# Token mixing in a two-block transformer kernel: convolution taps between POOL and ACT, six chunks on the raw input, scores placed later

## The chip, the cores and the metric

The kernel runs on one core of a Trainium2 chip. The core has five engines that work side by side, each through its own row of instructions in a fixed order: PE (matrix products), DVE (vector), ACT (scalar functions), POOL (general elementwise work) and SP, which here only issues loads. They wait for each other through semaphores. The time that counts is the device time of one execution in microseconds (us).

## What is computed

Two blocks follow each other. The first has two layers of: gated feed-forward, token mixing, gated feed-forward, each followed by a layer norm. It works on 272 tokens (16 learned ones and 256) of 1024 channels. The second block (attention and state mixing with modulation) is not touched by the change. The token mixing, with what matters here:

```python
def token_mix(h, w_in, pool_w, pool_scale, conv_dw, conv_db, conv_ln_g, conv_ln_b, conv_pw, ret_gn_g, w_out):
    z = h @ w_in                                   # 2816 columns
    xp, ca, cg, q, k, v, g = jnp.split(z, splits, axis=-1)
    y_pool = pool_mixer(xp, pool_w, pool_scale)    # trailing means over 2, 4, 8, 16 tokens, minus xp, times pool_w
    y_conv = conv_module(ca, cg, conv_dw, ...)     # ca * sigmoid(cg), causal 31-tap depthwise convolution, norm, silu, product
    y_ret = retention(q, k, v, g, ret_gn_g)        # 4 heads of 128, rotated q and k, decayed scores, head norm, gate
    return jnp.concatenate([y_pool, y_conv, y_ret], axis=-1) @ w_out
```

## The kernel before

Channels lie on the 128 partitions, tokens along the free axis; the state is eight tiles `st` of 128 channels. Each product is made three times in a reduced format: weights and inputs are split into a rounded high part and a rest, and PE adds high x high, high x low and low x high (lines 147 to 149 in `mm3`). A weight chunk of 1024 x 128 is loaded by SP into `raw` (L134), ACT casts it to `whi` (L140) and DVE subtracts to get `wlo` (L141). So one chunk on PE is 8 x 3 = 24 products of 272 columns. Four PSUM buffers take chunks (`mm_ps`, the pool `pmm`), four others scores and the like (`aux_ps`).

`token_mix` runs through 22 chunks of `w_in` in the order of `W_IN_KINDS`, two chunks for each entry. The first `RAWT` chunks come from `raw_tiles`: PE multiplies the state as it is, scaled by the layer norm's gain alone (two columns more carry the sums that the mean and the bias need), while statistics and the norm itself are still being made. What comes out of PSUM is then corrected: ACT copies the two columns to `wb` (L188), DVE subtracts the mean's part into `rz` (L190), POOL multiplies with the reciprocal deviation (L191), and the bias is added by the user of the tile. Beside it `ln_apply` makes the normalised input tile by tile: DVE `st` and `lnu` (L306, L308), ACT the high half of `xb` (L314), DVE the low half (L315), POOL the new state (L316). The other chunks come from `tiles` (PSUM tile `ps_g`) and multiply that normalised input; the first two of them share a sweep over its eight tiles.

What is done with a chunk: `ca` and `cg` make the convolution's input `cu` (POOL L584 and L587, ACT tanh L588, DVE L589). From then on `conv_tap` is called five times per chunk, with a lower priority. The convolution's two channel tiles are treated differently: t = 0 goes to DVE, one fused instruction for each tap (L442); t = 1 goes to POOL, one instruction for the product into a tile `tap` (L446) and one to add it to `cy` (L447). `q` and `k` are rotated in `rope_ret`: ACT copies the two halves exchanged into a tile `sw` (L424, L425), DVE multiplies twice and adds (L426 to L428). When a head's key is there, `ret_scores` makes its scores on PE (`ps_s`, L510) and DVE multiplies them with the decay (L511). `xp` is copied by ACT (L603) and then pooled in `pool_mix`, a generator of POOL instructions (L455 to L469) that is advanced twice per chunk, with two products at its end (`ps_pool`, L473). `v` and `g` are copied; after chunk 17 the values are transposed, the outputs `ps_o` made (L622), the convolution's norm and product follow in `conv_out`, and after chunk 21 the gates and transposes in `ret_out`. The eight chunks of `w_out` end the mixing.

A scheduler sets the order on each engine at build time, from the order in which the program is written, priorities, and when buffers come free. Short-lived tiles made by `self.t` (`tap`, `sw`, `rz`, `lnu`, `th`, `sq` and others) share one tag of six buffers: who takes a seventh waits until the last reader of one is done. An instruction that waits holds up all that stand behind it on its engine.

The module's constants that the change touches:

```python
RAWT = 4
W_IN_KINDS = (("ca", 256), ("cg", 512), ("q", 768), ("k", 1280), ("q", 1024), ("k", 1536), ("xp", 0),
              ("v", 1792), ("v", 2048), ("g", 2304), ("g", 2560))
```

Of the kernel before, what the change touches and what calls it, by code (L numbers as in the profile page):

```python
# [14 lines left out]
AF = mybir.ActivationFunctionType  # L15
ALU = mybir.AluOpType
AX = mybir.AxisListType
PSUM = bass.MemoryType.PSUM
# [21 lines left out]
RAWT = 4  # L40
LATE = 11
ACC = {"s": 0, "q": 1, "x0": 0, "x1": 2, "y": 0, "w": 1, "xw": 2}
W_IN_KINDS = (("ca", 256), ("cg", 512), ("q", 768), ("k", 1280), ("q", 1024), ("k", 1536), ("xp", 0),
# [45 lines left out]
class Ker:  # L89
# [61 lines left out]
    def gemm(self, items, X, cols, mark=0, tail=0):  # L151
        """items: (PSUM tile, weight chunk) pairs that share the sweep over the rows of X, but for the last `tail` rows."""
# [15 lines left out]
    def raw_tiles(self, srcs, ln, lead=2):  # L168
        """As tiles, of a layer norm's output, from its input scaled by the gain alone.

        Yields SBUF tiles that lack only the channel's bias, and the bias; the norm itself is made on the way."""
# [28 lines left out]
    def tiles(self, srcs, X, cols, kt=KD, lead=4, segs=None, hold=()):  # L200
        """Yields PSUM tiles of X @ w, one per 128-column chunk; the first `lead` share a sweep over X,
        one for each of segs, column ranges that become ready one after the other."""
# [23 lines left out]
    def mean_b(self, group, d, n, name, ps=None):  # L226
        """Mean over the channels of a group of tiles, the same in each partition."""
# [12 lines left out]
    def sqrt_table(self, after=None):  # L240
        """Have the square root's table in place before the chain that needs it."""
# [6 lines left out]
    def acc(self, S, key, m, src, n, eng):  # L248
        """Running sum over channel tiles; the eighth stays apart for the matmul that ends it."""
# [31 lines left out]
    def ln_raw(self, S, i, m, z, n):  # L281
        """Split of z times the gain of layer norm i, for raw_tiles."""
# [11 lines left out]
    def ln_start(self, S, i, eps, n, off, X):  # L294
        """Mean and reciprocal deviation, the same in each partition."""
# [5 lines left out]
    def ln_apply(self, S, i, eps, n, off, X, M, R, c):  # L301
        """State tile c <- its layer norm i; X gets the split of it."""
# [42 lines left out]
    def ada_cols(self, l):  # L345
        """Per-channel factors of layer l, [128, 8, 2] with the last axis (x, ctx)."""
# [16 lines left out]
    def ffn1(self, l, f, X, raw, n, off, ln):  # L363
        """SwiGLU; state <- 2 alpha state + ffn(state), and the sums of it."""
# [55 lines left out]
    def rope_ret(self, ps, dst):  # L420
        """dst <- ps * cos + halves swapped * signed sin, channels on partitions."""
# [131 lines left out]
    def token_mix(self, l, X, raw, n, off, ln):  # L553
# [25 lines left out]
        for c, z in enumerate(chain(self.raw_tiles(srcs[:RAWT], raw), self.tiles(srcs[RAWT:], X, slice(0, L1), lead=2))):  # L579
            kind, m = W_IN_KINDS[c // 2][0], c % 2  # L580
            if m == 0 and kind not in ("ca", "cg"):
                dst = self.hid2(kind)
# [1032 lines left out]
```

## Time and profile before

| | us |
|---|---|
| median of three runs (2161.81 to 2168.8) | 2165.63 |
| span of the profiled execution, first to last instruction | 2156.3 |
| median less that span | 9.3 |
| first layer's token mixing (218.1 to 350) | 131.9 |
| second layer's (752.2 to 882.5) | 130.3 |

The profiled execution's time is given by its span alone; what lies around it (start and end of the program) is taken from the median. Times on the profile's axis begin with the first instruction. An instruction's row names the engine, the line, what is written and read, and how long it took; its duration counts also what it waited for after its start, such as another engine's hold on the memory's ports. A wait is put down to the engine that came last. The granted clock of PE is shown as a share of its full speed.

### The profile page before, as it was taken

How to read it: one execution, taken by the hardware profiler on the slowest of the kernel's cores; microseconds unless marked ns; L12 is line 12 of the kernel's file. 1: busy time of each engine (PE TensorE's matmuls, PEld its weight loads, DVE VectorE, ACT ScalarE, POOL GpSimd, SP SyncE). 2: the span in 40 equal slices, each digit the busy share in tenths (PEclk: the TensorE clock that was granted, in tenths of full speed). 3: DMA queues.
4: the chain of work that ended last, by engine and by line, in shares of the span. 5: the costliest groups of instructions: out<-in, count | busy, mean ns of one | idle time of the engine just before them, and what ended most of it. 6: DMA issues, size and time to landing. Idle time of an engine off the chain costs nothing.

```text
span 2156.3 us, 37011 instructions
## 1 busy us (share of the span) xinstructions
PE 2088.8 (97%) x14486; PEld 1920.0 (89%) x14486; DVE 1575.5 (73%) x2554; ACT 1097.3 (51%) x1870; POOL 466.4 (22%) x500
## 2 busy tenths in 40 slices
PE   7999889999999989999999999999999998999998
PEld 7999889999999978999988788888888888789998
DVE  8889898989897789887755546685435558568873
ACT  6444446544554445654546656554324455566663
POOL 5002795202500288600200000310000013211000
PEclk9999999999999999999999999999999999999999
DMA  8877334787587724587522211133243232024653
GB/s 275 271 238 270 100 121 160 245 268 242 175 283 252 253 99 130 159 290 252 186 91 91 69 50 36 44 99 87 76 121 93 69 103 87 22 78 137 185 178 109
DMA packets 96079, 328.38 MB, mean 152 GB/s; under 512 B 10912, under 2 KB 13600, under 8 KB 95648
## 3 DMA queue, kind: packets, MB, share of 16 engines
q1 hardware_dynamic: 95328, 325.45, 47.0%
q8 instruction: 114, 1.87, 0.3%
q10 hardware_dynamic: 576, 0.56, 0.1%
q14 instruction: 61, 0.50, 0.1%
HBM read 324.92 MB, written 1.05 MB: 151 GB/s over the span
## 4 chain that ended last, share of the span: by engine, by line
PE 82%; POOL 8%; DVE 6%; issue 3%; ACT 2%; DMA 0%; DVEq 0%; POOLq 0%; ACTq 0%
PE ps_g L147 14%; PE ps_g L148 13%; PE ps_g L149 13%; PE ps_y L147 4%; PE ps_y L148 4%; PE ps_y L149 4%; PE ps_d L149 3%; PE ps_d L147 3%; POOL cy L447 3%; PE ps_d L148 3%; POOL tap L446 2%; PE ps_o L1049 2%; PE ps_s L1414 1%; PE ps_r L147 1%; PE ps_r L149 1%
## 5 line engine op out<-in xcount | busy, mean ns | idle before, releaser
L140 ACT CAST whi<-raw 128x1024 fp32r<-128x1024 f32 (+2 forms) x527 | 535.2, 1017 | 607.7 <-issue 174.1
L141 DVE TENSOR_TENSOR wlo<-raw,whi 128x1024 fp32r<-128x1024 f32 (+2 forms) x527 | 633.9, 1212 | 250.8 <-ACT whi L140 247.6
L147 PE MATMUL ps_g<-xb,whi 128*128 128x272 f32 (+2 forms) x2320 | 707.1, 307 | 8.6 <-DVE rz L190 4.6
L148 PE MATMUL ps_g<-xb,whi 128*128 128x272 f32 (+2 forms) x2320 | 707.0, 305 | 2.8 <-DVE xb L315 1.9
L149 PE MATMUL ps_g<-xb,wlo 128*128 128x272 f32 (+2 forms) x2320 | 708.4, 306 | 1.3 <-DVE wlo L141 1.3
L147 PEld LDWEIGHTS ps_g<-xb,whi 128*128 128x128 f32 x2320 | 439.1, 190 | 28.0 <-ACT xb L314 3.7
L148 PEld LDWEIGHTS ps_g<-xb,whi 128*128 128x128 f32 x2320 | 440.8, 190 | 22.3 <-DVE xb L315 3.7
L149 PEld LDWEIGHTS ps_g<-xb,wlo 128*128 128x128 f32 x2320 | 439.6, 190 | 19.4 <-DVE wlo L141 1.5
L147 PE MATMUL ps_y<-hid,whi 128*128 128x272 f32 (+1 forms) x704 | 207.8, 295 | 0.0
L341 DVE SCALAR_TENSOR_TENSOR junk<-ada,silu_c 128x1024 bf16<-128x1024 f32 x160 | 201.6, 1260 | 0.0
L148 PE MATMUL ps_y<-hid,whi 128*128 128x272 f32 (+1 forms) x704 | 201.4, 286 | 0.0
L149 PE MATMUL ps_y<-hid,wlo 128*128 128x272 f32 (+1 forms) x704 | 200.9, 285 | 0.0
L147 PEld LDWEIGHTS ps_y<-hid,whi 128*128 128x128 f32 x704 | 132.4, 188 | 8.8 <-issue 0.8
L148 PEld LDWEIGHTS ps_y<-hid,whi 128*128 128x128 f32 x704 | 132.9, 189 | 0.0
L149 PEld LDWEIGHTS ps_y<-hid,wlo 128*128 128x128 f32 x704 | 132.3, 188 | 0.0
L147 PE MATMUL ps_r<-xb,whi 128*128 128x274 f32 (+1 forms) x384 | 112.7, 294 | 9.7 <-ACT whi L140 9.7
L149 PE MATMUL ps_r<-xb,wlo 128*128 128x274 f32 (+1 forms) x384 | 111.4, 291 | 2.7 <-DVE wlo L141 2.7
L148 PE MATMUL ps_r<-xb,whi 128*128 128x274 f32 (+1 forms) x384 | 111.7, 291 | 0.0
L254 POOL TENSOR_TENSOR acc_s<-st,st 128x272 f32<-128x272 f32 (+1 forms) x6 | 10.1, 1684 | 463.0 <-DVE st L408 433.0
L793 POOL TENSOR_TENSOR xw<-st,yd 128x512 f32<-128x512 f32 (+1 forms) x10 | 11.5, 1145 | 346.5 <-ACT yd L789 346.5
L147 PEld LDWEIGHTS ps_r<-xb,whi 128*128 128x128 f32 x384 | 73.2, 191 | 10.3 <-issue 9.8
L222 ACT CAST hid<-hr 128x272 fp32r<-128x272 f32 (+1 forms) x110 | 45.4, 412 | 64.4 <-DVE hr L375 33.0
(407 smaller groups left out, 3910.9 us busy)
## 6 DMA issues: line engine op xcount, KB each, us to landing
raw<-in_w SPq DMA_DIRECT2D x236, 512.0 KB, 4.7
ada<-in_ada SPq DMA_DIRECT2D x96, 512.0 KB, 4.3
raw<-in_wup SPq DMA_DIRECT2D x88, 512.0 KB, 3.5
raw<-in_w_in SPq DMA_DIRECT2D x44, 512.0 KB, 3.6
raw<-in_w SPq DMA_DIRECT2D x32, 384.0 KB, 3.9
raw<-in_wdn SPq DMA_DIRECT2D x24, 384.0 KB, 3.1
raw<-in_w_out SPq DMA_DIRECT2D x16, 512.0 KB, 3.6
raw<-in_ev_in SPq DMA_DIRECT2D x16, 512.0 KB, 3.5
```

Of the source, the lines that this page charges most:

```text
L140: nc.scalar.copy(hi[:, :n], raw[:, :n])
L141: nc.vector.tensor_tensor(out=lo[:, :n], in0=raw[:, :n], in1=hi[:, :n].bitcast(F32), op=ALU.subtract)
L147: mm(ps, wh, xh, start=first, stop=False)
L148: mm(ps, wh, xl, start=False, stop=False)
L149: self.last = mm(ps, wl, xh, start=False, stop=last)
L222: self.nc.scalar.copy(hi, src)
L341: nc.vector.scalar_tensor_tensor(out=junk, in0=raw, scalar=1.0, in1=self.sc[:, s], op0=ALU.mult, op1=ALU.mult, accum_out=self.md[l][:, m, ...
L446: nc.gpsimd.tensor_scalar(out=p, in0=u[:, t, :L1 - s], scalar1=w, scalar2=0.0, op0=ALU.mult, op1=ALU.add)
L447: nc.gpsimd.tensor_tensor(out=y[:, t, s:], in0=y[:, t, s:], in1=p, op=ALU.add)
L793: nc.gpsimd.tensor_tensor(out=xw, in0=self.st[m][:, NM + sl.start:NM + sl.stop], in1=w[:, sl], op=ALU.mult)
L1049: nc.tensor.matmul(po[o][:, h * 64:(h + 1) * 64], pts[:, j * 128:(j + 1) * 128], vs(j, h), start=j == 0, stop=j == nj - 1)
L1414: nc.tensor.matmul(ps, qt[:96, h % 2, t * 128:(t + 1) * 128], kh[h % 2][:96], start=True, stop=True)
```

## The change

Four things change in the token mixing of both layers. The products of the 30 taps of t = 1 are made by ACT instead of POOL; POOL still adds them. The pooling branch `xp` moves from the 13th and 14th chunk to the 5th and 6th, and these two are made from the raw input (`RAWT` 6), with the bias added in ACT's copy. Since `q` and `k` are never raw, the branch for that goes. And the scores of a head are written into the program `DEFER` = 2 chunks after its key. Comments and docstrings are blanked elsewhere, without effect.

```diff
-RAWT = 4
+RAWT = 6
+DEFER = 2
...
-W_IN_KINDS = (("ca", 256), ("cg", 512), ("q", 768), ("k", 1280), ("q", 1024), ("k", 1536), ("xp", 0),
+W_IN_KINDS = (("ca", 256), ("cg", 512), ("xp", 0), ("q", 768), ("k", 1280), ("q", 1024), ("k", 1536),
               ("v", 1792), ("v", 2048), ("g", 2304), ("g", 2560))
...
             p = self.t(L1, "tap")[:, s:]
-            nc.gpsimd.tensor_scalar(out=p, in0=u[:, t, :L1 - s], scalar1=w, scalar2=0.0, op0=ALU.mult, op1=ALU.add)
+            nc.scalar.activation(p, u[:, t, :L1 - s], AF.Copy, scale=w)
             nc.gpsimd.tensor_tensor(out=y[:, t, s:], in0=y[:, t, s:], in1=p, op=ALU.add)
...
+            while late and late[0] <= c:
+                late.pop(0)
+                h = len(sT)
+                sT.append(self.ret_scores(h, q[h], k[h]))
...
             elif kind in "qk":
-                if isinstance(z, tuple):
-                    zb = self.t(L1, "zb")
-                    nc.scalar.activation(zb, z[0], AF.Identity, bias=z[1])
-                    z = zb
                 self.rope_ret(z, dst[:, m])
                 (q if kind == "q" else k).append(dst[:, m])
                 if kind == "k":
-                    sT.append(self.ret_scores(len(k) - 1, q[len(k) - 1], k[-1]))
+                    late.append(c + DEFER)
...
+            elif kind == "xp":
+                nc.scalar.activation(dst[:, m], z[0], AF.Identity, bias=z[1])
```

What the build makes of it, in three places of the first layer. Names carry their buffer number; the changed kernel's lines are its own, one to three higher.

PE before, in chunk 12 (`ps_g_3348`, a pooled chunk): `ps_s0_3274` and `ps_s1_3275` are the scores of head 2, whose key `k_3266` (first half) came from chunk 10.

```order
L147 MATMUL ps_g_3348<-xb2_83,whi_3351 128x272
L148 MATMUL ps_g_3348<-xb2_83,whi_3351 128x272
L510 MATMUL ps_s0_3274<-q_3171,k_3266 80x272
L510 MATMUL ps_s1_3275<-q_3171,k_3266 128x192
L149 MATMUL ps_g_3348<-xb2_83,wlo_3352 128x272
```

PE now, at the end of chunk 11 (`ps_g_3294`): the scores of head 0, whose key came from chunk 8.

```order
L149 MATMUL ps_g_3294<-xb6_87,whi_3297 128x272
L150 MATMUL ps_g_3294<-xb6_87,wlo_3298 128x272
L511 MATMUL ps_s0_3266<-q_3089,k_3164 80x272
L511 MATMUL ps_s1_3267<-q_3089,k_3164 128x192
L148 MATMUL ps_g_3294<-xb7_88,whi_3297 128x272
```

And PE now, between chunk 12 (`ps_g_3351`) and 13 (`ps_g_3412`): the pooled products `ps_pool`, which stood at the end of the mixing, are here.

```order
L149 MATMUL ps_g_3351<-xb7_88,whi_3354 128x272
L150 MATMUL ps_g_3351<-xb7_88,wlo_3355 128x272
L474 MATMUL ps_pool_3389<-py_3098,poolw_202 128x272
L511 MATMUL ps_s1_3327<-q_3089,k_3164 64x64
L474 MATMUL ps_pool_3395<-py_3098,poolw_202 128x272
L148 MATMUL ps_g_3412<-xb0_81,whi_3415 128x272
```

So a head's scores stand 2.9 chunks behind the chunk of its key instead of 1.3, and the pooled products stand between chunks.

ACT before, from chunk 12 on: only weight casts (`whi`) and copies out of PSUM stand here.

```order
L140 CAST whi_3564<-raw_3562 128x1024
L603 COPY xp_3379<-ps_g_3348 128x272
L140 CAST whi_3742<-raw_3740 128x1024
L603 COPY xp_3379<-ps_g_3392 128x272
L140 CAST whi_3777<-raw_3775 128x1024
```

ACT now, while chunks 7 to 10 are rotated (`sw`): tap products stand between the copies and ahead of weight casts.

```order
L447 ACTIVATE tap_3125<-cu_2705,vec_90 128x262
L447 ACTIVATE tap_3129<-cu_2705,vec_90 128x261
L425 COPY sw_3165<-ps_g_3133 64x272
L426 COPY sw_3165<-ps_g_3133 64x272
L141 CAST whi_3461<-raw_3459 128x1024
L447 ACTIVATE tap_3175<-cu_2705,vec_90 128x260
L447 ACTIVATE tap_3179<-cu_2705,vec_90 128x259
L447 ACTIVATE tap_3183<-cu_2705,vec_90 128x258
L425 COPY sw_3217<-ps_g_3186 64x272
L426 COPY sw_3217<-ps_g_3186 64x272
```

The products of taps have moved into ACT's row, each one with a buffer from the six.

POOL before, in the middle of the taps: products (L446) and adds (L447) take turns.

```order
L447 TENSOR_TENSOR cy_2706<-cy_2706,tap_3074 128x265
L446 TENSOR_SCALAR tap_3082<-cu_2705,vec_90 128x263
L447 TENSOR_TENSOR cy_2706<-cy_2706,tap_3078 128x264
L446 TENSOR_SCALAR tap_3132<-cu_2705,vec_90 128x262
L447 TENSOR_TENSOR cy_2706<-cy_2706,tap_3082 128x263
```

POOL now, in the same taps: `pw` and `py` are the pooling's tiles.

```order
L456 TENSOR_TENSOR pw2_3097<-pw1_3096 64x264
L457 TENSOR_SCALAR pw2_3097<-pw1_3096 64x8
L448 TENSOR_TENSOR cy_2706<-cy_2706,tap_3107 128x264
L448 TENSOR_TENSOR cy_2706<-cy_2706,tap_3111 128x263
L448 TENSOR_TENSOR cy_2706<-cy_2706,tap_3125 128x262
L448 TENSOR_TENSOR cy_2706<-cy_2706,tap_3129 128x261
L466 TENSOR_TENSOR py_3098<-pw1_3096,icnt_200 64x272
L468 TENSOR_TENSOR py_3098<-pw2_3097,icnt_200 64x272
```

The adds stay, the products are gone, and the pooling stands among the adds instead of behind them all.

## Rows read from the trace of the kernel before

**Rows 1.** The page: span, and section 1, busy time of each engine (share) xinstructions.

```profile
span 2156.3 us, 37011 instructions
PE 2088.8 (97%) x14486; PEld 1920.0 (89%) x14486; DVE 1575.5 (73%) x2554; ACT 1097.3 (51%) x1870; POOL 466.4 (22%) x500
```

**Rows 2.** Stretches of both mixings: length, busy time of each engine, clock, DMA.

```profile
core 0: us, PE busy (x) PEld busy (x) DVE busy (x) ACT busy (x) POOL busy (x), PEclk, DMA share, GB/s
218.10:350.00 131.90, 118.87 (x845) 110.47 (x845) 114.38 (x196) 70.64 (x127) 103.39 (x113) 0.96 0.38 123
...
233.60:255.30 21.70, 16.58 (x106) 14.67 (x105) 19.46 (x33) 12.13 (x22) 19.14 (x27) 0.92 0.27 83
...
269.90:284.40 14.50, 8.47 (x45) 7.27 (x43) 11.73 (x19) 3.90 (x7) 14.27 (x16) 0.76 0.32 113
284.40:297.80 13.40, 13.40 (x108) 13.37 (x107) 12.87 (x17) 5.33 (x8) 13.40 (x13) 1.00 0.61 201
...
325.90:350.00 24.10, 24.10 (x193) 24.10 (x193) 19.95 (x29) 16.47 (x30) 14.43 (x11) 1.00 0.51 173
...
752.20:882.50 130.30, 117.88 (x846) 109.68 (x846) 113.98 (x195) 70.30 (x127) 102.21 (x113) 0.95 0.40 124
```

**Rows 3.** Waits of PE in the two mixings: total us, times, longest.

```profile
PE ps_s L510 <- DVE k L428: 7.2, 2, 6.0
...
PE ps_ot L572 <- DVE yc L223: 0.5, 1, 0.5
...
PE ps_s L510 <- DVE k L428: 7.1, 2, 6.0
```

**Rows 4.** Waits of ACT in the first mixing.

```profile
ACT sw L424 <- POOL cy L447: 12.0, 3, 5.5
```

**Rows 5.** POOL's groups, 241 to 321: shapes xcount, busy us, mean ns, idle before.

```profile
L447 POOL TENSOR_TENSOR cy<-cy,tap 128x271 f32<-128x271 f32 (+29 forms) x30 | 32.8, 1093 | 0.5
L446 POOL TENSOR_SCALAR tap<-cu,vec 128x271 f32<-128x271 f32 (+29 forms) x30 | 29.4, 985 | 1.0 <-DVE cu L589 1.0
```

**Rows 6.** PE's groups, 218 to 350: the scores, and one of four layer statistics.

```profile
L510 PE MATMUL ps_s<-q,k 128*80 128x272 f32 (+2 forms) x24 | 6.2, 375 | 7.3 <-DVE k L428 7.2
...
L230 PE MATMUL ps_sq<-acc_q,mean 128*128 128x272 f32 x2 | 0.6, 392 | 0.0
```

**Rows 7.** ACT's groups, 218 to 350: instructions like the tap's product.

```profile
L290 ACT ACTIVATE xb<-st,vec 128x272 fp32r<-128x272 f32 x8 | 4.2, 523 | 3.6 <-DVE st L644 3.6
...
L262 ACT ACTIVATE sq<-st 128x272 f32<-128x272 f32 x8 | 3.3, 416 | 0.0
```

**Rows 8.** Single instructions in order of time, POOL and one of DVE.

```profile
261.90 0.74 POOL L447 TENSOR_TENSOR cy<-cy,tap 128x264 f32<-128x264 f32 x1
262.62 0.49 POOL L446 TENSOR_SCALAR tap<-cu,vec 128x262 f32<-128x262 f32 x1
...
283.26 5.41 POOL L446 TENSOR_SCALAR tap<-cu,vec 128x252 f32<-128x252 f32 x2
...
290.14 1.70 POOL L447 TENSOR_TENSOR cy<-cy,tap 128x251 f32<-128x251 f32 x1
...
292.44 0.89 POOL L447 TENSOR_TENSOR cy<-cy,tap 128x250 f32<-128x250 f32 x1
...
290.03 1.23 DVE L141 TENSOR_TENSOR wlo<-raw,whi 128x1024 fp32r<-128x1024 f32 x1 [0.21 <-ACT whi L140]
```

**Rows 9.** The pooling's first and last instruction on POOL (18 in all).

```profile
307.12 0.64 POOL L455 TENSOR_TENSOR pw<-xp 128x271 f32<-128x271 f32 x1
...
318.02 2.34 POOL L469 TENSOR_TENSOR py<-py,xp 128x272 f32<-128x272 f32 x1
```

**Rows 10.** DVE in order of time: start, us, idle before.

```profile
239.86 0.72 DVE L315 SCALAR_TENSOR_TENSOR xb<-lnu,vec,xb 128x272 fp32r<-128x272 f32 x1
240.79 0.44 DVE L589 SCALAR_TENSOR_TENSOR cu<-th,ca 128x272 f32<-128x272 f32 x1 [0.21 <-ACT th L588]
...
265.51 0.48 DVE L442 SCALAR_TENSOR_TENSOR cy<-cu,vec,cy 128x267 f32<-128x267 f32 x1
```

More of the change, by code (lines that the diff above doesn't have):

```diff
@@ L559, in token_mix @@
         q, k, vt, g, sT, xp = [], [], [], [], [], None
-        V, on = [], []
+        V, on, late = [], [], []
         taps, mix = [], None
```

## The prediction

> **What bounds the kernel now.** Read first the share of busy time: PE is busy 97% of 2156.3 us [rows 1], so a gain must come from stretches where PE waits. Next the table of stretches of the first token mixing (218.1 to 350): before 233.6 and from 284.4 on PE is nearly full; from 233.6 to 255.3 it is busy 16.6 of 21.7 us, and from 269.9 to 284.4 only 8.5 of 14.5, at a mean clock of 0.76, a mixture of the two levels 1.2 and 2.4 GHz [rows 2]. The second layer's mixing is a twin (130.3 us against 131.9). Then the waits: the score products wait 7.2 us for rotated keys, two waits in all, 7.1 us in the second layer [rows 3]. The keys are late because ACT's copy that starts a rotation waits 12.0 us for POOL's convolution adds [rows 4]. The copy's tile `sw` shares six buffers with the tap products, and a buffer comes free when POOL has added the product. POOL spends 29.4 us on 30 products and 32.8 us on 30 adds [rows 5], one product and one add in turn, until 307.1 [rows 9]. So between 250 and 285 the pacer is POOL, through buffers.
>
> How much PE loses: from 218.1 to the end of chunk 17 (297.8) 79.7 us pass. The products are 18 x 24 = 432. At the pace of the output stage, 192 products in 24.1 us or 0.1255 each [rows 2], they need 54.2 us; scores and layer statistics take some 7 (6.2 us busy in the score row and 2.4 in the four of statistics, of which one stands, less their overlap, an estimate) [rows 6]. That leaves **18.5 us lost per layer**, about 8.5 of it in the change from raw to normalised input, the rest around the scores. This is all that the change can fetch, some 37 us in two layers.
>
> **The change part by part.**
>
> *Tap products to ACT.* POOL loses 29.4 us per layer. ACT gets 30 instructions; an ACT instruction on 272 columns takes 0.416 us with no per-channel factor and 0.523 with one and a rounded output [rows 7]. I take 0.45 for 242 to 271 columns: 13.5 us per layer, between 12.5 and 15.7. ACT is busy 70.6 of 131.9 us [rows 2], so there is room; but ACT works in order, and each product needs one of the same six buffers. The buffers still come back only at the speed of POOL's adds. An add takes 0.74 us with DVE quiet, 0.89 beside conv taps on DVE, and 1.70 when it meets a `wlo` subtraction (DVE 290.03, 1.23 us) [rows 8]. The mean of 1.093 [rows 5] is my value. For DVE's `wlo`, twelve of which lie in the stretch, nothing changes.
>
> The Trainium skill ("SBUF — State Buffer", "Who interferes with whom") says that GpSimd and a VectorE instruction with two SBUF inputs exclude each other for a whole instruction. The add beside `wlo` agrees (0.74 to 1.70), the add beside two taps hardly (0.89); what it would make of the sum is a rival below.
>
> *Pooled input raw, and pooled early.* PE does the same 48 products, but at once after the gate's: the raw sweep lasts until 232.25 + 6.1 = 238.3, with no wait. In return two more tiles need a step on DVE and a scaling on POOL, some 0.5 each by instructions of like size [rows 8, 10], and ACT's copy takes a bias (0.523 [rows 7]), together some 2 us of work on POOL and ACT at the narrowest place. The pooling's 18 POOL instructions (307.1 to 320.4, 13.2 us [rows 9]) move from after the taps into their middle, and the two pooled products on PE from the tail to behind chunk 12. SP's row loads the second layer's `poolw` 12 loads earlier than before, into the buffer that the first layer's pooled products read: the weights of chunk 19 and after wait in SP's row behind them. PE asks for chunk 19 some five chunks, 15 us, after those products, so I take nothing; a product that is late by 5 us, as in R2, leaves 10.
>
> *Scores later.* By the order, head 0's scores stand 2.9 chunks behind the first key chunk; before it was 1.3 for the head that waited. The 1.6 chunks are 1.6 x 3.0 = 4.8 us of cover against waits of 7.2.
>
> *Walk along the new order, first layer.* All durations are those rows'.
> (a) Change of input. From 238.3 PE does 12 products on tiles 0 and 1 (239.8) and waits 0.8 for tile 2's low half (before: DVE 239.86 + 0.72 [rows 10]). Chunk 8 needs the PSUM buffer of raw chunk 4, whose read stands on DVE behind the gated product `cu` (240.79 + 0.44 [rows 10]) and four more instructions of 0.4 to 0.5: 243.5, a wait of 2.2. Normalised tile 5 stands on ACT behind the second pooled tile, which waits for POOL's scaling, and that stands behind four convolution adds: 245 + 4 x 0.9 to 1.09 + two state writes and a scaling of some 0.7 each + two ACT steps of 0.5, 251.7 to 252.5, a us later where one of them meets `wlo`, waits of 3.5 to 5 in all. Sum 6.5 to 8; I take 7.6, end 258.1.
> (b) Chunks 10 and 11 wait for the rotations' reads of chunks 6 and 7, behind five conv taps on DVE: 0.8 to 1.5 and 0.6; I take 1.7. 45 products later PE is at 265.4.
> (c) Head 0's scores: the key's copy needs a buffer from the eighth convolution add, which POOL reaches after half of the pooling at 263 to 266; rotation takes 3 more. Wait 1.1 to 4, I take 2.2. Head 1: 0.4.
> (d) The pooled products stand in the middle of PE's row. POOL then has left, from 254.5, when the three last state writes behind (a) are done: pooling 13.2, six adds 6.6, and a pause of 1.2 for ACT: 275.5; at the quiet prices 271, at the prices of 280 to 290 (DVE dense) 278.6. PE arrives at 273.6 to 274: wait 1.4 (0 to 4.8).
> (e) Head 2 behind chunk 14: the key's copy waits for the fifteenth add on ACT: 1.4 to 3, I take 1.6. Low halves of weights for chunks 15 and 16 behind the pooled split and rotations on DVE: 0.5 and 1.1 (up to 3 together).
> Sum of waits 7.6 + 1.7 + 2.2 + 0.4 + 1.4 + 1.6 + 1.6 = 16.5 where 18.5 were lost. The old figure has products at half clock in it; the new waits of 2 to 5 us are of the kind after which the granted clock fell, so I add 1.0: **17.5, a gain of 1.0**. In the tail the transposes' wait (0.5 [rows 3] and the start-up behind it, together 0.8) hides behind the output's first products; against it, the conv statistics wait for DVE's last taps, 0 to 2.5, for which I take 0.7. Per layer −1.1, both layers −2.2.
>
> The profiled span is 2156.3; the median of the runs is 2165.6, 9.3 more, which lies around the span. I let that stand: 2165.6 − 2.2 = **2163**.
>
> **The rivals.**
> *R1, POOL is really relieved.* If adds run at the quiet 0.74, pooling is done before PE asks (271) and keys are ready 4.8 us earlier: the 7.2 and 7.1 us score waits go, and the clock stays up. For it: the products were 29.4 of POOL's 62.2 us of convolution. Against: pooling's 13.2 us fall into the same stretch, and DVE is dense. About 8 us per layer: 2165.6 − 16 = 2150.
> *R2, the pooled product holds PE.* At the slow POOL prices (d) is 4.8, (c) 4, (e) 3 + 3, and chunk 17 ends 3 us later than before instead of 1 earlier; with the tail 5 per layer: 2175.6. It decides from a pooled tile written later than about 277. For it: two products beside dense DVE work took 5.41 us at 283.26, 0.49 each in quiet [rows 8]; against: while PE waits, DVE runs dry and POOL goes faster.
> *R3, strict exclusion of POOL and DVE.* If no POOL instruction overlapped one of DVE with two SBUF inputs, then from 243 on 37 us of POOL work (30 adds at 0.74, pooling at 11 in quiet, 4 of norm) and 41 of DVE's (29 taps at 0.48 [rows 10], 14 `wlo` at 1.23 [rows 8], rotations and norms 10) would follow each other: 321 for the last add, where it ends at 307.1 now [rows 9]; 2165.6 + 2 x 14 = 2194. The same sum for the kernel as it is, with 30 products at 0.49 more, gives 336, so the trace bears it out little. The Trainium skill's page "SBUF — State Buffer" states this rule in the section named above.
>
> **How the numbers follow.** A run of this kernel can tell 0.3% (6.5 us) from no change. Forecast 0.45 (own range 2155 to 2171), R1 0.28, R2 0.23, R3 0.04. Faster: all of R1 and 0.08 of the forecast, 0.36. Slower: R3 and most of R2, 0.24. Within: 0.40. The range of 2147 to 2178 leaves out R3 and the outer parts of R1 and R2, some 0.17. Bounds of the parts ((a) 1.5, (c) 3, (d) 4.8, (e) 4 us, twice) give the same width.
>
> **What would show it.** ACT's `sw` copies still wait for POOL's convolution adds, under 12.0 us but over 4 (forecast); near 0 would be R1. PE's wait of scores for keys falls from 7.2 to 2 to 5 per layer. A new wait of `ps_pool` for `py` on PE: 0 to 2 us forecast, 4 or more R2. Waits of normalised products for `rz` and `xb` stay near 6. POOL's adds stay near 1.0 us mean; 0.8 would speak for R1. ACT's tap instruction shows 0.42 to 0.52. The prediction is wrong if the time between the first raw product and the end of chunk 17, 79.7 us now, moves by more than 4 either way.

## The result: 13 us slower, at the time of a rival but by another way

The changed kernel takes 2176.41 us (median of 4 runs, 2174.26 to 2178.88), the kernel before, run beside it, 2163.72 (2161.26 to 2168.8): a ratio of 1.0062, 95% interval 1.0037 to 1.0087. (Ratios here are taken over the runs of both kernels, so they need not be the quotient of the medians.) The range held the time, but the forecast, no change or a little faster, was wrong.

The page of the changed kernel; the rows answer to [rows 1]:

```profile
span 2174.3 us, 37059 instructions
PE 2099.0 (97%) x14486; PEld 1931.2 (89%) x14486; DVE 1576.9 (73%) x2558; ACT 1122.8 (52%) x1934; POOL 404.1 (19%) x444
```

POOL is relieved by 62 us and ACT loaded with 25, as the change says, and the time rises. This execution took 2176.05 us as a whole, 1.8 more than its span; so the 9.3 that I had put around the span of before were mostly the difference between that execution and the median.

Where the loss lies: the two mixings take 139.3 and 138.0 us where they took 131.9 and 130.3, 15 of the 18 us between the two profiles. I cut the first mixing in three: until 240 chunk products are done (ten chunks), from there to the last transposition of values behind chunk 17, and the rest. The stretches of the kernel before (columns as in [rows 2]: length, busy PE, PEld, DVE, ACT, POOL, clock, DMA), cut in this way:

```profile
218.10:263.00 44.90, 38.49 (x261) 35.30 (x261) 38.40 (x65) 21.65 (x38) 32.90 (x42) 0.96 0.33 99
263.00:299.60 36.60, 30.51 (x220) 29.05 (x218) 31.58 (x48) 14.20 (x23) 36.29 (x35) 0.91 0.41 139
299.60:350.00 50.40, 49.87 (x369) 46.11 (x368) 44.39 (x84) 34.80 (x66) 34.21 (x38) 1.00 0.41 133
```

And of the changed kernel:

```profile
218.00:260.90 42.90, 36.61 (x249) 35.23 (x248) 35.05 (x55) 21.49 (x42) 26.79 (x38) 0.92 0.32 100
260.90:308.20 47.30, 37.13 (x234) 33.92 (x235) 41.43 (x64) 28.20 (x56) 30.59 (x36) 0.86 0.36 112
308.20:357.40 49.20, 48.82 (x366) 45.57 (x364) 38.32 (x81) 33.92 (x62) 14.46 (x11) 1.00 0.44 136
```

The first stretch, with the change of input, is 2.0 us shorter than before (no scores stand in it now), and the tail 1.2. The whole loss is in the middle, which grew from 36.6 to 47.3 us. There POOL, busy 36.3 of 36.6 us before, is busy 30.6 of 47.3, while DVE's work has grown from 31.6 to 41.4 us. This sum hides two parts:

```profile
262.90:282.00 19.10, 14.11 (x77) 12.22 (x76) 15.25 (x25) 11.58 (x25) 17.86 (x23) 0.82 0.29 95
282.00:299.00 17.00, 11.98 (x78) 11.21 (x78) 16.30 (x25) 10.52 (x23) 11.12 (x13) 0.80 0.20 54
```

Until 282 POOL is still the pacer, busy 17.9 of 19.1 us: from 261.3 to 277.0 the chain of work that ended last runs over its adds and the pooling among them, and ACT's copy of head 0's key waits 3.4 us for an add that stands behind half of the pooling. From 282 on POOL has time to spare (11.1 of 17.0), and DVE, busy 16.3, is what is long.

PE's waits in the first mixing (line waited for; us in total, times, longest); they answer to [rows 3]:

```profile
PE ps_s L511 <- DVE k L429: 3.7, 1, 3.7
PE ps_g L148 <- ACT xb L315: 3.5, 2, 2.8
PE ps_s L511 <- DVE rst L512: 3.2, 2, 2.9
PE ps_g L148 <- DVE rz L191: 2.5, 1, 2.5
PE ps_g L150 <- DVE wlo L142: 2.1, 1, 2.1
PE ps_g L148 <- DVE q L427: 1.4, 2, 1.0
```

One wait of 6 us has become five of 2 to 4. ACT's waits, the first and second answering to [rows 4]:

```profile
ACT sw L425 <- POOL cy L448: 3.8, 2, 3.4
ACT tap L447 <- POOL cy L448: 3.8, 2, 3.5
ACT whi L141 <- DMA raw<-in_w_in: 3.0, 2, 2.4
```

And the groups of POOL's adds and, below, of ACT's products, answering to [rows 5] (busy us, mean ns, idle before):

```profile
L448 POOL TENSOR_TENSOR cy<-cy,tap 128x271 f32<-128x271 f32 (+29 forms) x30 | 26.9, 897 | 8.2 <-ACT tap L447 4.6 <-DVE cy L443 1.7
```

```profile
L447 ACT ACTIVATE tap<-cu,vec 128x271 f32<-128x271 f32 (+29 forms) x30 | 13.7, 502 | 3.8 <-POOL cy L448 3.8
```

ACT's products cost 0.502 us each (I took 0.45), the adds fell from 1.093 to 0.897 us, and ACT's copies wait 3.8 us where they waited 12.0; ACT's products wait as much again.

### The profile page after: what moved, and what is told of

Read it like the earlier page. It is cut to its first block, busy times and chain, and to the rows that moved or that the text cites. A ratio compares the mean times of both kernels' runs of the same rounds, so it can differ in the third digit from the quotient of the medians.

```text
span 2174.3 us, 37059 instructions
## 1 busy us (share of the span) xinstructions
PE 2099.0 (97%) x14486; PEld 1931.2 (89%) x14486; DVE 1576.9 (73%) x2558; ACT 1122.8 (52%) x1934; POOL 404.1 (19%) x444
## 4 chain that ended last, share of the span: by engine, by line
PE 82%; DVE 6%; POOL 5%; issue 5%; ACT 2%; DMA 0%; DVEq 0%; POOLq 0%; ACTq 0%
PE ps_g L148 14%; PE ps_g L149 14%; PE ps_g L150 14%; PE ps_y L148 4%; PE ps_y L149 3%; PE ps_y L150 3%; PE ps_d L150 3%; PE ps_d L148 3%; PE ps_d L149 3%; PE ps_o L1052 2%; PE ps_s L1417 1%; PE ps_s L1103 1%; PE ps_tt L1245 1%; PE ps_pt L1041 1%; POOL rz L192 1%
## 5 line engine op out<-in xcount | busy, mean ns | idle before, releaser
L150 PE MATMUL ps_g<-xb,wlo 128*128 128x272 f32 (+2 forms) x2288 | 700.8, 307 | 5.4 <-DVE wlo L142 5.4
L148 PE MATMUL ps_r<-xb,whi 128*128 128x274 f32 (+1 forms) x416 | 122.1, 294 | 8.9 <-ACT whi L141 8.9
L150 PE MATMUL ps_r<-xb,wlo 128*128 128x274 f32 (+1 forms) x416 | 120.9, 291 | 2.7 <-DVE wlo L142 2.7
L149 PE MATMUL ps_r<-xb,whi 128*128 128x274 f32 (+1 forms) x416 | 121.2, 291 | 0.0
L148 PEld LDWEIGHTS ps_r<-xb,whi 128*128 128x128 f32 x416 | 79.3, 191 | 9.5 <-issue 9.1
L150 PEld LDWEIGHTS ps_r<-xb,wlo 128*128 128x128 f32 x416 | 78.9, 190 | 3.5 <-DVE wlo L142 3.5
L149 PEld LDWEIGHTS ps_r<-xb,whi 128*128 128x128 f32 x416 | 79.2, 190 | 0.3
```

Source lines behind the costliest of these rows:

```text
L148: mm(ps, wh, xh, start=first, stop=False)
L149: mm(ps, wh, xl, start=False, stop=False)
L150: self.last = mm(ps, wl, xh, start=False, stop=last)
```

## The experiments

Three parts are told apart: A, the tap products on ACT; B, the pooling branch as fifth and sixth chunk on the raw input; C, the scores two chunks later. "Before" was run beside each kernel; its medians were 2161.3 to 2163.7.

| kernel | parts | median us | ratio to before | 95% interval |
|---|---|---|---|---|
| a_taps_on_act, a_again | A | 2150.0, 2149.7 | 0.9936, 0.9950 | 0.9911 to 0.9961, 0.9933 to 0.9968 |
| ac_defer | A, C | 2151.0 | 0.9943 | 0.9923 to 0.9964 |
| a_tap4_out18 | A, 4 taps a chunk, norm later | 2156.1 | 0.9976 | 0.9966 to 0.9985 |
| a_tap4 | A, 4 taps a chunk | 2159.2 | 0.9994 | 0.9983 to 1.0005 |
| a_raw_q | A, six raw chunks | 2164.1 | 1.0013 | 0.9998 to 1.0028 |
| c_defer | C | 2164.3 | 1.0003 | 0.9990 to 1.0015 |
| a_tap4_out19 | A, 4 taps, norm later still | 2165.2 | 1.0017 | 1.0007 to 1.0026 |
| abc_late_mix | A, B without early pooling, C | 2165.3 | 1.0024 | 1.0013 to 1.0036 |
| a_early_xp | A, branch early but not raw | 2168.1 | 1.0036 | 1.0022 to 1.0049 |
| abc_late_prod | A, B with late products, C | 2171.3 | 1.0042 | 1.0026 to 1.0058 |
| ab_no_defer | A, B | 2172.2 | 1.0038 | 1.0015 to 1.0061 |
| the changed kernel | A, B, C | 2176.4 | 1.0062 | 1.0037 to 1.0087 |
| b_early_pool | B | 2181.9 | 1.0089 | 1.0068 to 1.0110 |
| bc_no_act | B, C | 2188.7 | 1.0117 | 1.0102 to 1.0133 |
| a_share6 | A, six of DVE's taps on ACT and POOL | 2189.5 | 1.0122 | 1.0100 to 1.0144 |

### Which part costs

Only the tap products, `a_taps_on_act`:

```diff
-            nc.gpsimd.tensor_scalar(out=p, in0=u[:, t, :L1 - s], scalar1=w, scalar2=0.0, op0=ALU.mult, op1=ALU.add)
+            nc.scalar.activation(p, u[:, t, :L1 - s], AF.Copy, scale=w)
```

> The kernel before with one edit: ACT makes the 30 tap products of t = 1, everything else (order of chunks, raw part of four chunks, scores) as before. Theory 1 (the early pooling on raw input is what costs; it fills POOL's free time with pooling and adds longer waits at the change of input): the tap products themselves are good, the copies' wait for POOL (12.0 us per layer) falls under 5, each mixing takes 126 to 130 us instead of 131.9 and 130.3, time 2153 to 2160. Theory 2 (the tap products in ACT's row cost, since copies and weight casts stand behind them): mixing 135 to 139, time 2172 to 2180.

Measured: 2150.0, some 12 us faster than before. Theory 1 had the sign, and the gain is larger than it said (3 us below its range); theory 2 falls. The same kernel again, for a second profile:

> The kernel before with ACT's tap products alone, once more, for a second profile: its first six times lay between 2143.7 and 2157.0, with a mean granted clock of 0.983 to 0.989, and the execution that was profiled was the slowest. If the spread is the clock's, a faster execution shows the same waits within 2 us in all and fewer products at the lower level (in the mixing or elsewhere), about 1 us of time for each 0.0009 of mean clock. Time 2147 to 2153.

Measured: 2149.7. Waits of PE, then of ACT, in its first mixing:

```profile
PE ps_s L510 <- DVE k L428: 5.9, 2, 3.2
```

```profile
ACT sw L424 <- POOL cy L447: 2.2, 2, 1.8
```

The copies' wait for POOL, 12.0 us before, is 2.2: with its products gone POOL holds the copies up little, and the longest score wait falls from 6.0 to 3.2 us (all score waits for keys from 7.2 to 5.9). The two profiles have spans of 2155.2 and 2147.8 us at mean clocks of 0.985 and 0.988, so 7.4 us for 0.003 of clock, about twice the time that I had expected for it. The six executions of the first series ran from 2143.7 us at a clock of 0.989 to 2157.0 at 0.985, with one at 0.983 taking 2153.4: the clock goes with the spread, but not tightly, and the first mixing is alike in both profiles (130.6 and 131.0 us) while the second is 129.1 and 126.6. A single profile of this kernel is therefore good to some 5 us, and the verdicts here rest on medians. Of the 12 us the profiles show a part: the two mixings together are 2.5 and 4.6 us shorter than before. What follows the second mixing, which no edit of this study touches, took between 1270.6 and 1278.9 us in the 17 profiles (1273.8 before, 1275.9 and 1270.6 in these two). Where the rest of A's gain lies is not shown.

Only the early branch, `b_early_pool`:

```diff
-RAWT = 4
+RAWT = 6
...
-("cg", 512), ("q", 768), ("k", 1280), ("q", 1024), ("k", 1536), ("xp", 0),
+("cg", 512), ("xp", 0), ("q", 768), ("k", 1280), ("q", 1024), ("k", 1536),
...
+            elif kind == "xp":
+                nc.scalar.activation(dst[:, m], z[0], AF.Identity, bias=z[1])
```

> The kernel before with one edit: the pooling branch as the fifth and sixth raw chunk; POOL still makes the tap products, scores as before. Theory 1: POOL has 62 us of convolution and 13 us of pooling before the last keys, keys and pooled products come later still, each mixing takes 139 us or more (the changed kernel has 139.3), time 2178 to 2200. Theory 2: no ACT products, so nothing is lost; time 2160 to 2168, mixing 130 to 133.

Measured: 2181.9, 20 us slower; mixings of 144.0 and 142.1. Theory 1. In its middle stretch POOL is full again, 47.7 of 48.8 us (columns as above):

```profile
262.50:311.30 48.80, 37.27 (x233) 33.18 (x232) 37.70 (x62) 17.15 (x30) 47.71 (x60) 0.86 0.31 90
```

Only the later scores, `c_defer`:

```diff
+            while late and late[0] <= c:
+                late.pop(0)
+                h = len(sT)
+                sT.append(self.ret_scores(h, q[h], k[h]))
...
-                    sT.append(self.ret_scores(len(k) - 1, q[len(k) - 1], k[-1]))
+                    late.append(c + DEFER)
```

> The kernel before with one edit: scores of a head written two chunks after its key. Theory 1 and 2 alike: the wait of 6.2 us of one score group for its key falls to 0 to 3 us, each mixing gains 1 to 4 us, time 2156 to 2164. A rival, theory 3 (the later scores cost, since the four PSUM buffers of scores then hold PE up behind DVE's decay products, a wait of 3.2 us in the changed kernel): a new wait of scores for the decay product of 3 us or more, mixing unchanged or longer, time 2164 to 2172.

Measured: 2164.3, no difference. The wait for keys is nearly gone, and its place is taken by the wait for DVE's decay product, which frees a PSUM buffer of scores:

```profile
PE ps_s L511 <- DVE rst L512: 8.2, 3, 4.6
...
PE ps_s L511 <- DVE k L429: 0.6, 1, 0.6
```

Before, 7.2 us were waited for keys; now 8.2 and 0.6. Theory 3 named the wait rightly; the time it gave covered this result at its lower end, and theories 1 and 2 missed it by 0.3 us at their upper end.

B and C with POOL's products, `bc_no_act`, the changed kernel with the product line put back:

```diff
-            nc.scalar.activation(p, u[:, t, :L1 - s], AF.Copy, scale=w)
+            nc.gpsimd.tensor_scalar(out=p, in0=u[:, t, :L1 - s], scalar1=w, scalar2=0.0, op0=ALU.mult, op1=ALU.add)
```

> The changed kernel with the tap products back on POOL, so early pooling and later scores without ACT's products. Theory 1: as the changed kernel or slower, mixing 139 or more, time 2176 to 2195. Theory 2: the loss goes, mixing 130 to 133, time 2155 to 2166.

Measured: 2188.7, the slower side of theory 1. ACT's products are worth 12 us in the changed kernel as well.

A and C, `ac_defer`, is `c_defer` with the product line of `a_taps_on_act`. A and B, `ab_no_defer`, is the changed kernel with the scores written at their key:

```diff
-                    late.append(c + DEFER)
+                    sT.append(self.ret_scores(len(k) - 1, q[len(k) - 1], k[-1]))
```

> ACT's tap products and the later scores, with four raw chunks and the order of chunks as before. Theory 1e (the raw, early pooling branch carries all of the loss; the later scores are worth nothing either way, as alone, 2164.3 against 2161.8): 2147 to 2154. Theory 3 (the later scores cost where ACT makes the products, since scores of two heads then meet in the four PSUM buffers behind DVE's decay products): 2157 to 2166, waits of scores for the decay product of 3 us or more per layer.

> The changed kernel with the scores written at their key, as before. Theory 1e: as the changed kernel, 2172 to 2179. Theory 3: 2160 to 2169, and the waits of scores for the decay product (3.2 and 4.5 us in the two layers) are gone.

Measured: 2151.0 and 2172.2. With A alone the later scores change nothing; in the changed kernel they cost some 4 us at most (2172.2 against 2176.4, with intervals that overlap). Beside B without A they cost more: 2188.7 (`bc_no_act`, 2188.1 to 2189.2) against 2181.9 (`b_early_pool`, 2181.0 to 2185.3). The two waits of PE for `rst` in the first mixing are 0.6 us in `ab_no_defer` and 3.2 in the changed kernel. So theory 1e holds in the main: the parts nearly add up, A −10 to −13 (−12 alone), B +20 to +25 (+22 and +25 on top of A), C 1 to 2 with the branch late, which is within the noise, and 4 to 7 with it early.

### What in the early branch costs

`a_raw_q`: `a_taps_on_act` with a longer raw part and nothing moved, so that two q chunks are raw.

```diff
-RAWT = 4
+RAWT = 6
```

> The kernel before with ACT's tap products and with six raw chunks, but the order of chunks as before: the fifth and sixth raw chunk are the first q chunks (the branch that the kernel before has for raw q adds the bias on ACT). Nothing is pooled early. Theory 1a (of the early pooling branch it is the pooling on POOL and its product that cost): as with ACT's products alone, 2146 to 2156. Theory 1b (two more raw chunks make the change of input costly: one wait of 2.6 and one of 3.0 us instead of some of 0.3 to 1.4, each with half clock behind it): 2160 to 2172.

Measured: 2164.1, 14 us more than A alone: theory 1b. The stretches of its first mixing, and then those of `a_again`:

```profile
217.50:264.20 46.70, 39.42 (x250) 38.00 (x249) 36.45 (x61) 23.77 (x46) 23.95 (x32) 0.85 0.30 91
264.20:300.60 36.40, 32.61 (x232) 30.35 (x231) 34.47 (x55) 25.51 (x50) 31.99 (x28) 0.95 0.46 145
300.60:350.20 49.60, 49.60 (x370) 46.30 (x368) 41.21 (x84) 35.40 (x66) 24.73 (x26) 1.00 0.44 133
```

```profile
217.40:262.20 44.80, 38.91 (x253) 36.25 (x253) 39.72 (x62) 25.65 (x48) 25.34 (x34) 0.90 0.36 107
262.20:297.60 35.40, 32.14 (x227) 30.11 (x226) 31.73 (x51) 22.55 (x43) 31.64 (x33) 0.94 0.41 122
297.60:348.40 50.80, 49.65 (x369) 46.33 (x368) 43.40 (x85) 35.16 (x66) 19.79 (x17) 1.00 0.48 139
```

The change of input lasts 1.9 us longer at a clock of 0.85, and DVE has done 3.3 us less by its end, which it does in the next stretch. Over both layers the profiled mixings differ by 4 and 6 us from the two profiles of A; the rest of the 14 I could not find, and it stays open.

`a_early_xp`: `a_taps_on_act` with the branch early, but not raw.

```diff
-("cg", 512), ("q", 768), ("k", 1280), ("q", 1024), ("k", 1536), ("xp", 0),
+("cg", 512), ("xp", 0), ("q", 768), ("k", 1280), ("q", 1024), ("k", 1536),
```

> The kernel before with ACT's tap products and the pooling branch as fifth and sixth chunk, but four raw chunks: the pooling branch is the first pair on normalised input. The pooling's POOL work stands among the convolution's adds. Theory 1a: 2162 to 2176, PE waits for keys of 5 us or more per layer. Theory 1b: as with ACT's products alone, 2146 to 2156.

Measured: 2168.1: theory 1a as well. Both halves of the branch cost; I had taken them for alternatives. The middle stretch:

```profile
258.00:304.40 46.40, 36.87 (x236) 33.34 (x235) 44.14 (x69) 26.59 (x51) 30.91 (x34) 0.89 0.40 124
```

DVE is busy 44.1 of 46.4 us, POOL only 30.9, and the chain that ended last has no instruction of POOL in it there. So it is DVE that is full here, though the early branch itself needs little of DVE.

`abc_late_mix`: the changed kernel, with the pooling begun after chunk 13.

```diff
             if kind == "xp" and m == 1:
-                mix = self.pool_mix(l, dst, Y)
+                xp = dst
+            if c == 13:
+                mix = self.pool_mix(l, xp, Y)
```

> The changed kernel, but the pooling of its early, raw pooling branch begins only after chunk 13, as in the kernel before, so that its POOL instructions and products stand behind the taps again. Theory 1a: the score waits shorten, 2150 to 2162. Theory 1b: the change of input is as in the changed kernel (waits of 2.6 and 3.0 us), 2170 to 2178.

Measured: 2165.3, 11 us of the loss gone, 15 above A alone. `abc_late_prod`: POOL's work early, but PE's products, ACT's scaling and the split behind them only after chunk 17, where the generator now waits:

```diff
+        while not self.pool_go:
+            yield
         for t in range(2):
             ps = self.aux_ps("ps_pool")[:, :L1]
...
+            self.pool_go = c >= 17
             if kind == "xp" and m == 1:
```

> The changed kernel with the pooling's POOL instructions where they are (early, among the convolution's adds), but the two pooled products on PE, with ACT's scaling and the split on ACT and DVE behind them, written after chunk 17 instead of when the pooling is done. Theory 1c (the pooling costs by POOL's time: its 13 us stand ahead of adds, which return the buffers that the rotations' copies wait for): 2172 to 2178, nothing gained. Theory 1d (it costs by the product's place: its split stands in DVE's row ahead of a weight's low half that PE then waits 2.2 us for, and the second layer's poolw load stands in SP's row): 2163 to 2170, as with late pooling.

Measured: 2171.3, between the two theories: some 5 of the 11 us go with the place of the product and what follows it, 6 with the place of the pooling on POOL. The step of 5 is not clear by the intervals of the table, which overlap, but the profiled mixings have both steps: 277.3 us for two layers in the changed kernel, 272.6 in `abc_late_prod`, 266.9 in `abc_late_mix`. Middle stretches, first of `abc_late_mix`, then of `abc_late_prod`:

```profile
259.80:298.90 39.10, 33.29 (x231) 30.68 (x231) 38.15 (x60) 27.15 (x54) 33.57 (x37) 0.96 0.40 123
```

```profile
261.20:304.20 43.00, 32.17 (x232) 29.23 (x231) 40.87 (x61) 26.62 (x52) 28.60 (x33) 1.00 0.40 123
```

The product itself was not waited for in the changed kernel: its last pooled tile was begun at 276.86 and took 0.77 us, and PE came at 280.2. What its place costs is the split, which stands in DVE's row ahead of a weight's low half that PE needs (start, us):

```profile
286.72 0.96 DVE L429 TENSOR_TENSOR k<-k,sw 128x272 f32<-128x272 f32 x1
287.61 1.83 DVE L224 TENSOR_TENSOR yc<-ys,yc 128x272 fp32r<-128x272 f32 x2
289.36 1.73 DVE L142 TENSOR_TENSOR wlo<-raw,whi 128x1024 fp32r<-128x1024 f32 x1
```

PE stood from 289.1 to 291.1 for this `wlo`. The low half also frees the weight's buffer: SP's next load was issued at 291.15, and ACT's cast waited 2.4 us for it.

**The middle stretch's length goes with DVE's work in it** in these seven kernels in which ACT makes the products: 28.5 us of DVE in 31.3 (`a_tap4`, below), 31.7 in 35.4 (`a_again`), 34.5 in 36.4 (`a_raw_q`), 38.2 in 39.1 (`abc_late_mix`), 40.9 in 43.0 (`abc_late_prod`), 44.1 in 46.4 (`a_early_xp`), 41.4 in 47.3 (the changed kernel, with ACT's waits for POOL on top). Over the whole mixing DVE does about the same, 112 to 116 us; it is the share in the middle that grows. The lengths alone do not say which of the two sets the other, since a stretch between two points of PE's row that grows for any reason also takes in more of DVE's row; for DVE speak the chains that ended last (no POOL in those of `a_early_xp`, `abc_late_mix` and `abc_late_prod`), its busy share of 88 to 98%, and `a_tap4`, where taps were taken out and the stretch fell. In the changed kernel DVE's row is the bound in the second part only, as shown above. Groups of DVE in the middle stretch of the changed kernel:

```profile
L142 DVE TENSOR_TENSOR wlo<-raw,whi 128x1024 fp32r<-128x1024 f32 x11 | 14.9, 1350 | 0.6 <-ACT whi L141 0.6
L443 DVE SCALAR_TENSOR_TENSOR cy<-cu,vec,cy 128x264 f32<-128x264 f32 (+15 forms) x16 | 10.4, 648 | 0.0
L428 DVE TENSOR_TENSOR sw<-sw,rcs 128x272 f32<-128x272 f32 x8 | 5.2, 656 | 0.0
L429 DVE TENSOR_TENSOR q<-q,sw 128x272 f32<-128x272 f32 x4 | 3.8, 951 | 0.0
...
L429 DVE TENSOR_TENSOR k<-k,sw 128x272 f32<-128x272 f32 x4 | 3.5, 885 | 0.0
```

And of `a_again`, with eight low halves and five rotations:

```profile
L141 DVE TENSOR_TENSOR wlo<-raw,whi 128x1024 fp32r<-128x1024 f32 x8 | 12.1, 1518 | 0.0
L442 DVE SCALAR_TENSOR_TENSOR cy<-cu,vec,cy 128x264 f32<-128x264 f32 (+15 forms) x16 | 11.2, 702 | 0.2
...
L427 DVE TENSOR_TENSOR sw<-sw,rcs 128x272 f32<-128x272 f32 x5 | 3.0, 609 | 0.0
L428 DVE TENSOR_TENSOR k<-k,sw 128x272 f32<-128x272 f32 x3 | 1.8, 602 | 0.0
L428 DVE TENSOR_TENSOR q<-q,sw 128x272 f32<-128x272 f32 x2 | 1.4, 688 | 0.0
```

The second and third step of the rotations take 12.5 us against 6.2, the low halves 14.9 against 12.1, the pooled split adds 1.8; both kernels have 16 taps there.

In the order of before the two pooling chunks stood between the last key and the values: 48 products, 6 us of PE, that ask nothing of DVE but two low halves, while the last rotations, decay products and taps drained. The change takes this pause away and puts all eight rotations into the middle, where five had been left. This reading rests on where DVE's work lies in the orders and traces; a kernel that gives DVE such a pause back and changes nothing else was not run.

### Is DVE's row the bound that is left?

`a_tap4`: `a_taps_on_act`, with four taps written per chunk.

```diff
-                for _ in range(5):
+                for _ in range(4):
                     if taps:
```

> The kernel before with ACT's tap products and four taps written per chunk instead of five, so that fewer of VectorE's taps stand among the rotations. If DVE's row is what makes the keys late now (with ACT's products DVE is busy over 90% between 240 and 285): a gain on ACT's products alone, 2138 to 2147, score waits under 4 us per layer where they are 5.7. If it is POOL's adds: no difference, 2146 to 2154, or some us more, since the taps end later and the convolution's statistics wait for them (1.2 us in each layer now).

Measured: 2159.2, some 5 us above the second range, as the end of that expectation allows. The middle stretch did fall, to 31.3 us, as DVE's row would have it; the tail took it all back:

```profile
262.50:293.80 31.30, 29.81 (x224) 28.30 (x225) 28.46 (x45) 22.00 (x42) 28.87 (x26) 1.00 0.43 132
293.80:349.80 56.00, 51.31 (x369) 47.45 (x368) 47.03 (x89) 35.38 (x66) 26.18 (x26) 0.94 0.42 127
```

```profile
PE ps_mean L230 <- DVE cy L442: 4.7, 1, 4.7
```

The second fence is from PE's waits: the convolution's statistics wait 4.7 us for the last taps. So I wrote the norm later, after chunk 18 (`a_tap4_out18`) and after chunk 19 (`a_tap4_out19`):

```diff
-            if c == 17:
+            if c == 18:
                 while taps:
                     self.conv_tap(l, u, cy, *taps.pop(0))
                 self.conv_out(l, cy, Y)
```

> ACT's tap products alone, four taps per chunk, and the convolution's norm written after chunk 18 instead of 17, one chunk (3 us) later on PE. With four taps per chunk the stretch of the scores fell from 35.3 to 31.3 us, and the statistics' wait for the last taps grew from 1.1 to 4.6 us and more. If these two are what they seem: mixing 126 to 128 us, time 2143 to 2152, below both kernels. If DVE's work only comes later and holds up the end of the mixing: 2155 to 2162.

> The same with the convolution's norm after chunk 19, so 6 us later on PE. If the statistics' wait was all: mixing 125 to 127, time 2141 to 2150. If the chain behind the statistics (norm, silu, product, split) then ends after the first output products need it: a new wait at the convolution's product or the first output chunk of 2 to 5 us, time 2150 to 2160.

Measured: 2156.1 and 2165.2. After chunk 19 the statistics no longer wait, but the convolution's product does, and for longer:

```profile
PE ps_pw L497 <- ACT cz L491: 6.1, 1, 6.1
```

The rival in each expectation, then; in the second the time and the wait (2160 and 5 us at most) came out above what it gave. The taps are a fixed amount of DVE work between two ends; spreading them moves the wait from the keys to the norm. Last, `a_share6` gives DVE's last six taps to ACT and POOL:

```diff
-        elif t == 0:
+        elif t == 0 and j > 5:
```

> ACT's tap products alone, and the last six of VectorE's 30 taps handed to ACT and POOL as well, which relieves DVE's row of some 4 us per layer just where the convolution's statistics wait for it (1.1 us of PE, 6.1 of ACT). If DVE ends the chain there: 2143 to 2149, and the statistics' wait gone. If POOL's six more adds beside the pooling come later than DVE's taps did: a wait of the statistics for POOL of 2 us or more, 2150 to 2158.

Measured: 2189.5, worse than either expectation. Values wait for ACT, whose row now holds products that wait for buffers, one of them 6.8 us; the adds that free these stand behind the pooling in POOL's row (287.60 to 300.18):

```profile
PE ps_v L522 <- ACT v L603: 5.6, 1, 5.6
PE ps_o L622 <- ACT vv L524: 5.4, 1, 5.4
```

The best kernel of the study is A alone, 2149.7 us, 0.5 to 0.6% under the kernel before.

## Why the prediction was wrong, by its steps

**The step that failed** is the last sum of the walk, "16.5 where 18.5 were lost", with 1.0 for the clock: it sets waits alone against a loss that was not waits alone, and it takes the products at the lower clock level at a fifth of what they cost. This is the time from the first raw product to the end of chunk 17, taken apart in the traces by the distances between the starts of PE's instructions (a wait is what a distance with idle time in it has above a product's own 0.1255 us; second layer in brackets, each figure rounded by itself):

| us | forecast | before | changed |
|---|---|---|---|
| 432 products at full pace | 54.2 | 54.2 (54.2) | 54.2 (54.2) |
| waits | 16.5 | 14.2 (13.1) | 18.0 (18.8) |
| chunk products at the lower level, above that pace | 1.0 | 1.6 (2.4) | 5.7 (4.8) |
| scores, statistics, pooled products, starts after waits | 7.0 | 9.8 (9.5) | 10.4 (10.6) |
| sum | 78.7 | 79.8 (79.3) | 88.4 (88.5) |

Of the 18.5 us that I called lost, 14.2 were waits. Against these the 16.5 of the walk already say a loss of 2.3, not a gain. The time moved by 8.7 us, more than the 4 that the prediction named as its sign of being wrong.

**The clock: the term that was mis-sized most.** I allowed 1.0 us for products at the lower level. By the granted clock 57 chunk products of the changed kernel stand there until the end of chunk 17, and 16 of the kernel before; such a product starts 0.227 us after the one ahead, not 0.126. The products behind head 0's wait, 273.7 to 277.5 (busy us, mean ns):

```profile
L148 PE MATMUL ps_g<-xb,whi 128*128 128x272 f32 x6 | 2.8, 470 | 0.0
```

And the same product at the full level, 282 to 287.7:

```profile
L148 PE MATMUL ps_g<-xb,whi 128*128 128x272 f32 x16 | 4.8, 301 | 0.0
```

**The waits.** In the sum they came out near, 18.0 for 16.5. At the change of input 2.6 + 0.2 + 0.8 + 3.0 = 6.7 us, where I had 7.6; 0.5 + 1.2 for the rotations' reads, exactly the 1.7 forecast. Head 0's scores: forecast 2.2, measured 3.9, by the way that (c) describes: the key's copy waited for the eighth add, which ended at 268.1 behind half of the pooling. Pooled products: 1.4 and none (a score between them 0.5). Head 2's scores: 1.6 and 3.2, not for its key but for the PSUM buffer that `rst` frees. Low halves: 1.6 and 2.2.

**The tap products.** That POOL paced the stretch through the shared buffers was right, and A shows it: 12.0 us of waiting become 2.2. But the step from there, that the buffers "still come back only at the speed of POOL's adds" and so little is won, was wrong for A by itself, which is worth 12 us. The products were half of the time in which POOL made one buffer free. R1 gave 2150, and that is what A alone takes, but this is luck: R1 was of the whole change, with adds at 0.74 us and no score waits left, and in A alone the adds take 1.02 to 1.06 and the score waits are 5.7 to 5.9 us.

**The price of the early branch.** I charged it to POOL and to the change of input, and took DVE's part for nothing beyond two more steps; by the experiments it costs 22 to 25 us on top of A. What I did not ask is what stood in the old place. The pause behind the last key was work that covered DVE; that its loss is the cause rests on the orders and traces, not on a run.

**The rivals.** R2 gave 2175.6 and the time was 2176.4, but not by its mechanism, and its own terms do not give that time: set into the sum, they stand 8.0 us above the forecast's, which is 7 later per layer and not 3. The pooled tile was done at 277.6, about where R2 would decide, and PE came 2.6 us after it, having lost its time at head 0. R3 falls: it had the last add of the first mixing at 321, and in the changed kernel the last nine begin at 286.46 and take 8.60 us:

```profile
286.46 8.60 POOL L448 TENSOR_TENSOR cy<-cy,tap 128x250 f32<-128x250 f32 x9 [1.05 <-ACT tap L447]
```

The rule of the Trainium skill that it was weighed with ("SBUF — State Buffer", "Who interferes with whom") agrees with the adds' mean of 0.897 us being above the quiet 0.74, but taken strictly it would have given that late end. The sum that weighed R3 against the kernel before also counts 11 us of pooling that stand behind the last add there; without them it gives 325, still 18 us above the 307.1 of the trace.

**The reading of one profile.** The execution of before that was profiled, with its span of 2156.3 (some 2158 as a whole, if 1.8 us lie around it as in the changed kernel), is at the lower end of what that kernel takes (fifteen others in one series: 2158.97 to 2174.12), and the 9.3 us around it were mostly chance. It cost the forecast nothing, since I added a difference to the median, but the two profiles show 18 us where the medians show 13.

## What to carry to other kernels

Before moving a piece of work, ask what its old place gave to the others: a stretch that needs little of a nearly full engine is that engine's pause, and is missed when it goes. Measure the parts of a composite change apart; here one was worth −12 us, one +22 to +25, and the sum hid both. When an engine is relieved, look at who is next by adding up the work per stretch, not over the whole, and cut the stretch until one engine is full in each piece: DVE was at 73% of the span and at 88 to 98% of the stretch that mattered, and in the changed kernel POOL was still the pacer of that stretch's first part. And when new waits are set against an old loss, both must be counted in the same way.

## What the runs showed of the hardware

Several waits of 2 to 4 us cost more than one of 6, because products ran at the lower clock level behind them: in the first mixing of the changed kernel the granted clock was at the lower level for 20.5 us, in four stretches, each beside or right behind a wait with 2 to 4 us of idle time, and 57 chunk products ran there; in the kernel before, with one wait of 6.0 us and small ones, it was 10.2 us and 16 products (second layer 17.1 us and 48 products against 13.7 and 24). Executions of one kernel (A alone) differ by 13 us, at mean clocks from 0.983 to 0.989. What follows the second mixing, the same program in all kernels, took 1270.6 us with 31 us at the lower level and 1278.9 with 52. And a product of up to 271 columns with a per-channel factor took ACT 0.50 us in the mean of 30 where POOL, beside a dense DVE, took 0.985.
